# Three pairs of feed-forward blocks per half computed by seven products instead of eight, interleaved with ordinary blocks

## The chip, the core and the metric

The kernel runs on one core of one Trainium2 chip. The metric is device time of one execution in microseconds (us). Engines are named as in the profile: PE multiplies (its weight loads are shown as PEld), DVE, ACT and POOL compute on 128 partitions, SP only issues transfers.

## What is computed

A decoder trunk of two layers over 512 tokens of width 1024. Each layer adds a mixing block (three kinds of token mixer with gates), and then a feed-forward block:

```python
for l in range(DEPTH):
    h = rms_norm(x, mix_norm_g[l])
    ...                                   # three mixers, gated, merged
    x = x + merged @ w_o[l]
    h = rms_norm(x, ffn_norm_g[l])
    x = x + (jax.nn.silu(h @ ffn_w1[l]) * (h @ ffn_w3[l])) @ ffn_w2[l]
```

The feed-forward block's inner width is 2816 = 22 blocks of 128. Everything is float32.

## The kernel before

Activations stand with features on partitions and the 512 tokens along the free side, so one matrix product of a 128x128 weight block with an activation chunk is one matmul of 512 columns. Float32 accuracy comes from splitting every operand into a high and a low part, both in the reduced format fp32r: `split` (L99) makes the high part on ACT (L100) and the low part, source minus high, on DVE or POOL (L101). `mm3` (L111) then issues three matmuls per 128-block: high by high (L113), high by low (L114), low by high (L115). `weights` (L103) loads a raw weight tile of up to 512 columns (four blocks) through SP into one of 3 `wr` buffers and splits it into `wh` and `wl` (4 buffers each); it does so at a raised priority of 90 places, so that loads and splits run ahead of the matmuls. `gemm_gen` (L121) runs one output block over all its input blocks and yields after every second one; `gemm_fm` runs it through. Which instruction goes next on an engine is set at build time by a list scheduler that takes, among those it holds ready, the one traced first; on the chip each engine then works through its list in order.

`ffn` (L1031) works in two halves of 11 inner blocks (`HH`). For each block it runs a product with `w1` (24 matmuls: 8 input blocks by 3) and one with `w3` (24), multiplies the first by the norm factor `rb` (L339), applies tanh on ACT (L1044), two fused operations on DVE (L1045, L1046, the second with `rb` again), multiplies by the `w3` product (L1049), and splits the result into the tiles that `w2` reads. After 11 blocks come 8 products with `w2` (33 matmuls each) whose results are added to `x` (L1055). The norm factor itself is computed late: the sums of squares are reduced by PE behind the first `w1` product (L317) and spread by four transposes in `norm_end` (L331). POOL does nothing in this stage. Ahead of it, `layer` runs the eight output products of `w_o` (24 matmuls each) with `x` updated at L1232, and `norm_chunk` (L299) scales, splits and squares each finished chunk.

PSUM has 8 banks: 2 called `mm`, 2 `s`, 3 `t`, 1 `o`. In this stage an `mm` request takes banks of the first three kinds in turn (`WIDE`). SBUF buffers are counted by tag in `bufs` (L74); `e` and `P3` have 3 each, `big` 6.

Of the kernel before, what the change touches and what calls it, by code (L numbers as in the profile page):

```python
# [19 lines left out]
D, S, L, KC, NT = 1024, 512, 2, 8, 4  # L20
# [4 lines left out]
FFN, HC, HH = 2816, 22, 11  # L25
# [38 lines left out]
class Builder:  # L64
    def __init__(self, ctx, tc, io, layers=L, dbg=None):
        self.tc, self.nc, self.io, self.layers = tc, tc.nc, io, layers
        self.dbg = dbg or {}
        nc = self.nc
        self.V, self.A, self.T = nc.vector, nc.scalar, nc.tensor
        pool = lambda n, b=1, **k: ctx.enter_context(tc.tile_pool(name=n, bufs=b, **k))  # L70
        self.cst, self.sb, self.sm = pool("cst"), pool("sb"), pool("sm", 2)
        self.psum = pool("psum", 1, space=PSUM)
        self.n = 0
        self.bufs = dict(wr=3, wh=4, wl=4, h=16, mg=8, oT=8, cq=10, qk=8, v=8, big=6, pt=5, P0=2, P1=2, P2=2, P3=3, e=3)  # L74
        self.pending = False
        self.pbufs = dict(mm=2, s=2, t=3, o=1)
        self.wide, self.turn = False, 0
        self.weng, self.debt, self.mid = None, 0.0, False
# [287 lines left out]
    def add(self, gen, us, due):  # L366
        self.fillers.append([gen, us, due])
# [641 lines left out]
    def rglru(self, l, fill):  # L1009
# [18 lines left out]
        while outs:  # L1028
            self.rg_out(l, *outs.pop(0))

    def ffn(self, l, x, out_chunk):  # L1031
        V, A, io = self.V, self.A, self.io
        tags = ["oT"] * 8 + ["cq"] * 7 + ["qk"] * 7
        for half in range(2):
            hid = []
            for c in range(HH):
                hc = half * HH + c
                ps1 = self.gemm_fm(io["w1"][l, hc], self.h)
                if c == 0 and half == 0:
                    self.norm_stats()  # L1040
                    ps = self.gemm_fm(io["w3"][l, hc], self.h)
                u = self.rs_mul(ps1)
                th = self.pg("e")
                A.activation(th, u, AF.Tanh, scale=0.5)  # L1044
                V.scalar_tensor_tensor(u, th, 1.0, u, OP.add, OP.mult)  # L1045
                V.scalar_tensor_tensor(u, u, 0.5, self.rb, OP.mult, OP.mult)  # L1046
                if c or half:
                    ps = self.gemm_fm(io["w3"][l, hc], self.h)
                V.tensor_tensor(u, ps, u, OP.mult)  # L1049
                hi, lo = self.pg(tags[2 * c], F32R), self.pg(tags[2 * c + 1], F32R)  # L1050
                self.split(hi, lo, u)
                hid.append((hi, lo))
            for oc in range(KC):
                ps = self.gemm_fm(io["w2"][l, half, oc], hid)
                V.tensor_tensor(x[oc], ps, x[oc], OP.add)  # L1055
                if half == 1:
                    out_chunk(oc, x[oc])

    def run(self):
        nc, V, A, io = self.nc, self.V, self.A, self.io  # L1060
# [17 lines left out]
    def layer(self, l):  # L1078
        nc, V, A, io = self.nc, self.V, self.A, self.io
# [128 lines left out]
        for h in range(1, 8):  # L1208
            g = 48 + 3 * h - 2
# [26 lines left out]
        if not last:
            self.vectors(l + 1)
# [65 lines left out]


def build(d, layers=L, dbg=None):
    nc = bacc.Bacc("TRN2", target_bir_lowering=False, num_devices=1)
    io = {k: nc.dram_tensor(k, v.shape, mybir.dt.from_np(v.dtype), kind="ExternalInput").ap() for k, v in d.items()}
    io["out"] = nc.dram_tensor("out", (KC, 128, S), F32, kind="ExternalOutput").ap()
    io["xs"] = nc.dram_tensor("xs", (KC, 128, S), F32, kind="Internal").ap()
    for k, s in (dbg or {}).items():  # L1310
        io[k] = nc.dram_tensor(k, s, F32, kind="ExternalOutput").ap()
    with tile.TileContext(nc) as tc, ExitStack() as ctx:
        b = Builder(ctx, tc, io, layers, dbg)
        b.run()
    return nc
# [9 lines left out]
```

## Time and profile before

| | us |
|---|---|
| median of 3 runs | 1986.11 (1983.62 to 1986.47) |
| the profiled execution | 1982.81 |
| its span in the trace | 1981.0 |
| PE busy in the span | 1935.6 |
| DVE, ACT, POOL busy | 1319.7, 996.6, 252.0 |

The span is what the trace covers; the remaining 1.8 us of that execution lie around it. A PE row's duration runs from its start to the end of its drain, so that matmuls overlap in the rows; the pace of PE is read from the distances between starts.

### The profile page before, as it was taken

The numbers are of one execution on the slowest core, as the hardware profiler recorded it, in microseconds if no ns is written. First come the engines' busy times: TensorE is split into PE (matmuls) and PEld (weight loads), VectorE is DVE, ScalarE is ACT, GpSimd is POOL, SyncE is SP. The second block draws the span as 40 slices with busy tenths as digits, with TensorE's granted clock in tenths as the row PEclk, the third lists the DMA queues.
The fourth block names the chain that finished last, engine by engine and source line by source line (L and its number), as shares of the span: only waits on it lengthen the run. The fifth ranks groups of instructions, "written<-read, shape, count | busy, mean of one in ns | idle before, by whom it ended". The sixth has DMA issues, their size and how long they took to land.

```text
span 1981.0 us, 26967 instructions
## 1 busy us (share of the span) xinstructions
PE 1935.6 (98%) x9472; PEld 1627.8 (82%) x9472; DVE 1319.7 (67%) x2783; ACT 996.6 (50%) x1937; POOL 252.0 (13%) x232
## 2 busy tenths in 40 slices
PE   9898999999999999999999899999999999999999
PEld 8777878888888888888888688888888888888887
DVE  8689998788545554455556999878874465534542
ACT  5466776687334332233344577857773343323331
POOL 0453442000000000000004536310000000000000
PEclk9999999999999999999999999999999999999999
DMA  5211101223333223323432111113233322333333
GB/s 159 86 56 34 41 31 43 87 94 104 109 125 101 96 96 93 99 98 96 131 112 93 43 41 44 38 46 100 95 102 119 121 91 100 96 94 99 97 102 100
DMA packets 100519, 173.94 MB, mean 88 GB/s; under 512 B 11936, under 2 KB 26144, under 8 KB 100384
## 3 DMA queue, kind: packets, MB, share of 16 engines
q1 hardware_dynamic: 100384, 172.22, 27.3%
q8 instruction: 74, 1.21, 0.2%
q14 instruction: 61, 0.50, 0.1%
HBM read 167.98 MB, written 4.19 MB: 87 GB/s over the span
## 4 chain that ended last, share of the span: by engine, by line
PE 78%; DVE 8%; ACT 2%; issue 1%; POOL 0%; ACTq 0%; DVEq 0%; POOLq 0%
PE pst L114 9%; PE pst L113 9%; PE pst L115 9%; PE psmm L113 8%; PE psmm L114 8%; PE psmm L115 8%; PE pss L114 7%; PE pss L113 7%; PE pss L115 7%; PE pst L660 1%; DVE P L645 1%; DVE pss L633 1%; PE pso L673 1%; PE pso L674 1%; ACT P L636 1%
## 5 line engine op out<-in xcount | busy, mean ns | idle before, releaser
L100 ACT ACTIVATE wh<-wr 128x512 fp32r<-128x512 f32 (+3 forms) x640 | 387.5, 608 | 698.4 <-PE pst L114 261.0
L101 DVE TENSOR_TENSOR wl<-wr,wh 128x512 fp32r<-128x512 f32 (+2 forms) x526 | 355.1, 676 | 247.5 <-ACT wh L100 242.4
L101 POOL TENSOR_TENSOR wl<-wr,wh 128x512 fp32r<-128x512 f32 (+2 forms) x114 | 138.8, 1224 | 951.8 <-ACT wh L100 935.8
L113 PE MATMUL psmm<-h,wh 128*128 128x512 f32 x600 | 237.2, 395 | 3.7 <-ACT wh L100 2.8
L115 PE MATMUL psmm<-h,wl 128*128 128x512 f32 x600 | 235.2, 392 | 0.6 <-POOL wl L101 0.6
L114 PE MATMUL psmm<-h,wh 128*128 128x512 f32 x600 | 235.0, 392 | 0.0
L113 PE MATMUL pst<-h,wh 128*128 128x512 f32 x512 | 199.8, 390 | 0.0
L114 PE MATMUL pst<-h,wh 128*128 128x512 f32 x512 | 199.3, 389 | 0.0
L115 PE MATMUL pst<-h,wl 128*128 128x512 f32 x512 | 199.3, 389 | 0.0
L113 PEld LDWEIGHTS psmm<-h,wh 128*128 128x128 f32 x600 | 112.9, 188 | 26.4 <-ACT wh L100 3.2
L113 PE MATMUL pss<-h,wh 128*128 128x512 f32 x344 | 134.2, 390 | 0.0
L115 PE MATMUL pss<-h,wl 128*128 128x512 f32 x344 | 133.9, 389 | 0.0
L114 PE MATMUL pss<-h,wh 128*128 128x512 f32 x344 | 133.9, 389 | 0.0
L115 PEld LDWEIGHTS psmm<-h,wl 128*128 128x128 f32 x600 | 112.9, 188 | 24.6 <-POOL wl L101 1.1
L114 PEld LDWEIGHTS psmm<-h,wh 128*128 128x128 f32 x600 | 112.9, 188 | 20.8
L636 ACT ACTIVATE P<-pss,nm 128x512 f32<-128x512 f32 x192 | 100.1, 525 | 55.4 <-DVE nm L633 32.3
L113 PEld LDWEIGHTS pst<-h,wh 128*128 128x128 f32 x512 | 96.1, 188 | 20.2 <-ACT e L984 0.4
L115 PEld LDWEIGHTS pst<-h,wl 128*128 128x128 f32 x512 | 96.1, 188 | 20.1
L114 PEld LDWEIGHTS pst<-h,wh 128*128 128x128 f32 x512 | 96.1, 188 | 19.8
L633 DVE CUSTOM_DVE_ANT_0 pss<-pss,mask 128x512 f32<-128x512 f32 x192 | 93.7, 489 | 7.2 <-PE pss L115 5.8
L660 PE MATMUL pst<-ident,P 128*128 128x128 f32 x480 | 76.6, 274 | 11.5 <-DVE P L645 5.3
L660 PEld LDWEIGHTS pst<-ident,P 128*128 128x128 f32 x480 | 58.2, 141 | 28.1 <-issue 17.8
(423 smaller groups left out, 4303.4 us busy)
## 6 DMA issues: line engine op xcount, KB each, us to landing
wr<-w SPq DMA_DIRECT2D x240, 256.0 KB, 2.6
wr<-wfm SPq DMA_DIRECT2D x188, 256.0 KB, 2.6
wr<-wpc SPq DMA_DIRECT2D x32, 256.0 KB, 2.6
wr<-wo SPq DMA_DIRECT2D x32, 256.0 KB, 2.6
wr<-wb SPq DMA_DIRECT2D x32, 192.0 KB, 2.4
wr<-w SPq DMA_DIRECT2D x32, 192.0 KB, 2.3
mg<-xT SPq DMA_DIRECT2D x16, 256.0 KB, 2.7
wr<-wpa SPq DMA_DIRECT2D x16, 256.0 KB, 2.6
```

The lines of the kernel that those rows point to most:

```text
L100: self.A.activation(hi, src, AF.Copy)
L101: (eng or self.V).tensor_tensor(lo, src, hi.bitcast(F32), OP.subtract)
L113: mm(ps, a[0], b[0], start=first, stop=False)
L114: mm(ps, a[0], b[1], start=False, stop=False)
L115: mm(ps, a[1], b[0], start=False, stop=last)
L633: self.V.tensor_tensor_reduce(p[:, :W], p[:, :W], self.mask[:, 512 - W:], 1.0, 3e38, OP.add, OP.min, j.nm[:, i:i + 1])
L636: self.A.activation(j.Pi[i], p[:, :128 * (i + 1)], AF.Exp, bias=j.nm[:, i:i + 1], scale=-1.0, accum_out=j.l[:, i:i + 1])
L645: V.tensor_scalar(j.Pi[i], j.Pi[i], j.gate[:, i:i + 1], j.l[:, i:i + 1], op0=OP.mult, op1=OP.mult)
L660: self.T.transpose(ps[:, c:c + 128], j.Pi[i][:, kt * 128:kt * 128 + 128], self.ident)
L673: T.matmul(o[:, 512 - n:], j.V[kt], h[:, m0:m0 + n], start=j.first and kt == 0, stop=False)
L674: T.matmul(o[:, 512 - n:], j.V[kt], l_[:, m0:m0 + n], start=False, stop=j.last and kt == NT - 1)
```

## The change

Six of the 11 inner blocks of each half are taken as three pairs, each pair with both of its products (`w1` and `w3`) computed by the Strassen-Winograd scheme: the weight is cut into 2x2 parts (two inner blocks by two halves of the 8 input blocks) and the activations into 2x2 parts (two halves of the input blocks by two halves of the tokens), and seven products of 4 blocks by 256 tokens take the place of eight. A pair takes 7 products x 2 matrices x 4 blocks x 3 matmuls = 168 matmuls of 256 columns, where it took 96 of 512. The weight sums `s1` to `s4` are made on POOL, the activation sums `t1` to `t4` on DVE and POOL while `w_o` still runs (`x_scaled`, `x_sums`), and the seven results are combined on DVE as they leave PSUM. The steps of a pair are interleaved with the steps of the five ordinary blocks: one step of an ordinary product (6 matmuls of 512), one step of a pair (12 of 256). The last `w3`-side use of the norm factor moves behind `w2`: the hidden tile is left without it, and each `w2` result is multiplied by `rb` before it is added to `x`. Buffers: `wh` and `wl` 5 each, a new tag `cf`, and the hidden tiles lie under other tags; a smaller scratch area makes room.

```diff
-        self.bufs = dict(wr=3, wh=4, wl=4, h=16, ...
+        self.bufs = dict(wr=3, cf=3, wh=5, wl=5, h=16, ...
+LAS = 2
+DUO_BANKS = ("s", "t", "s", "t", "t")
...
+    def x_sums(self, k, x, g):
+        V, P = self.V, self.nc.gpsimd
+        h, g1 = self.hg[k], g[:, k + 4:k + 5]
+        a, b = slice(0, 256), slice(256, 512)
+        t13, t24 = self.pg("pt"), self.pg("pt")
+        P.tensor_tensor(t13[:, a], h[:, b], h[:, a], OP.subtract)
+        V.scalar_tensor_tensor(t13[:, b], x[:, b], g1, h[:, b], OP.mult, OP.subtract)
+        P.tensor_tensor(t24[:, a], t13[:, b], h[:, a], OP.add)
+        V.scalar_tensor_tensor(t24[:, b], x[:, a], g1, t24[:, a], OP.mult, OP.subtract)
...
+        for t, e in ((t13, V), (t24, P)):
+            hi, lo = self.pg("qk", F32R), self.pg("oT", F32R)
+            self.split(hi, lo, t, e)
...
+    def duo_events(self, srcs):
...
+            ev += [(o - 8, load, o, "r21", "big"), (o - 8, load, o, "r22", "P3"), (o - 7, load, o, "r11", "big"),
+                   (o - 5, add, o, "s1", "r21", "r22", OP.add), (o - 4, load, o, "r12", "big"),
+                   (o - 4, add, o, "s3", "r11", "r21", OP.subtract, "r21"),
+                   (o - 1, add, o, "s2", "s1", "r11", OP.subtract, "r11"),
+                   (o + 2, add, o, "s4", "r12", "s2", OP.subtract, "s2")]
...
+    DUO = (("r11", "b11"), ("s2", "t2"), ("r12", "b21"), ("s1", "t1"), ("s3", "t3"), ("s4", "b22"), ("r22", "t4"))
...
+                ps = self.ps(DUO_BANKS[(7 * u + i) % 5])
+                for m in range(2):
+                    emit(n * u + 2 * i + m)
+                    wh, wl = splits.pop((u, 2 * i + m))
+                    for k in range(4):
+                        s = slice(k * 128, k * 128 + 128)
+                        self.mm3(ps[:, m * 256:m * 256 + 256], (wh[:, s], wl[:, s]), X[xn][k], k == 0, k == 3)
+                    if m == 0:
+                        yield
+                if name == "r11":
+                    A.activation(t1, ps, AF.Copy)
+                elif name == "s2":
+                    V.tensor_tensor(t2, ps, t1, OP.add)
...
+                if name in ("s4", "r22"):
+                    q = int(name == "r22")
+                    late.append(lambda q=q, u=u, f=(f1, f2)[q]: done(u, q, f))
+                yield
...
+    def duo_split(self, splits, key, w, name):
+        hi, lo = self.pg("wh", F32R), self.pg("wl", F32R)
+        self.split(hi, lo, w[name], self.nc.gpsimd if key[1] in (7, 9, 11) else None)
...
+        def hidden(hc, w1, w3, v=lambda t: t):
...
+            V.tensor_tensor(u, w1, v(self.rb), OP.mult)
+            A.activation(th, u, AF.Tanh, scale=0.5)
+            V.scalar_tensor_tensor(u, th, 1.0, u, OP.add, OP.mult)
+            V.scalar_tensor_tensor(u, u, 0.5, w3, OP.mult, OP.mult)
+            A.activation(v(hi), u, AF.Copy)
+            V.tensor_tensor(v(lo), u, v(hi).bitcast(F32), OP.subtract)
...
+        def mix(g, c):
+            while next(c, self) is not self:
+                next(g, None)
+            self.drain(g)
+
+        def down(half, oc):
+            ps = self.gemm_fm(io["w2"][l, half, oc], [self.hid[c] for c in range(HH)])
+            t = self.pg("cf", F32, [128, 2, 512])[:, 0]
+            V.tensor_tensor(t, ps, self.rb, OP.mult)
+            (V if half else self.nc.gpsimd).tensor_tensor(x[oc], x[oc], t, OP.add)
...
+            g = pairs([o + 5, o + 7, o + 9])
+            c = singles(range(o, o + 5))
...
+            self.hid = {}
+            for _ in range(4):
+                next(c)
+            mix(g, c)
...
+            self.x_scaled(oc, t, self.ffng)
+            if oc > 3:
+                self.x_sums(oc - 4, t, self.ffng)
```

## Rows read from the trace of the kernel before

**Rows 1.** The page: span, busy time by engine, chain that ended last by engine.

```profile
span 1981.0 us, 26967 instructions
...
PE 1935.6 (98%) x9472; PEld 1627.8 (82%) x9472; DVE 1319.7 (67%) x2783; ACT 996.6 (50%) x1937; POOL 252.0 (13%) x232
...
PE 78%; DVE 8%; ACT 2%; issue 1%; POOL 0%; ACTq 0%; DVEq 0%; POOLq 0%
```

**Rows 2.** Busy time by stretch (w_o; feed-forward of layers 0 and 1).

```profile
596.00:640.00 44.00, 44.00 (x196) 36.42 (x195) 26.22 (x40) 19.89 (x32) 0.00 (x0) 1.00 0.32 105
645.00:1019.00 374.00, 374.00 (x1673) 311.75 (x1672) 189.46 (x303) 125.60 (x203) 0.00 (x0) 1.00 0.33 105
1622.00:1980.00 358.00, 355.21 (x1573) 293.91 (x1571) 171.99 (x269) 109.52 (x176) 0.00 (x0) 1.00 0.31 98
```

**Rows 3.** PE in order: start, duration; feed-forward of layer 0, first and last.

```profile
639.54 0.39 PE L113 MATMUL pst<-h,wh 128*128 128x512 f32 x1
...
644.75 0.39 PE L115 MATMUL pst<-h,wl 128*128 128x512 f32 x1
644.98 0.95 PE L317 MATMUL pso<-ones,e 128*128 128x1 f32 x8
...
1000.01 0.33 PE L113 MATMUL pst<-wh,h 128*128 128x384 f32 x1
```

**Rows 4.** PE in order: twelve matmuls of 256 columns, and the next.

```profile
278.32 0.28 PE L113 MATMUL psmm<-wh,cq 128*128 128x256 f32 x1
278.44 0.28 PE L114 MATMUL psmm<-wl,cq 128*128 128x256 f32 x1
...
279.75 0.40 PE L113 MATMUL pss<-qk,qk 96*128 96x512 f32 x1
```

**Rows 5.** Weight loads of the same stretch, in order.

```profile
278.44 0.19 PEld L115 LDWEIGHTS psmm<-wh,cq 128*128 128x128 f32 x1
...
279.51 0.19 PEld L115 LDWEIGHTS psmm<-wh,cq 128*128 128x128 f32 x1
```

**Rows 6.** DVE groups of the feed-forward of layer 0: busy us, mean ns.

```profile
L101 DVE TENSOR_TENSOR wl<-wr,wh 128x512 fp32r<-128x512 f32 x134 | 89.9, 671 | 81.7 <-ACT wh L100 79.8 <-PE pso L331 2.0
L1045 DVE SCALAR_TENSOR_TENSOR e<-e,e 128x512 f32<-128x512 f32 x22 | 15.2, 693 | 4.6 <-ACT e L1044 4.5
L1046 DVE SCALAR_TENSOR_TENSOR e<-e,rsb 128x512 f32<-128x512 f32 x22 | 15.2, 692 | 0.7
...
L339 DVE TENSOR_TENSOR e<-psmm,rsb 128x512 f32<-128x512 f32 x8 | 5.5, 691 | 10.8 <-PE psmm L115 10.8
```

**Rows 7.** ACT groups of the same stretch.

```profile
L100 ACT ACTIVATE wh<-wr 128x512 fp32r<-128x512 f32 x134 | 82.9, 619 | 217.6 <-PE pst L114 90.4 <-PE pss L114 64.1 <-PE psmm L114 59.1
L1044 ACT ACTIVATE e<-e 128x512 f32<-128x512 f32 x22 | 13.9, 634 | 8.8 <-DVE e L339 8.8
```

**Rows 8.** POOL groups of the whole span, by shape.

```profile
L101 POOL TENSOR_TENSOR wl<-wr,wh 128x512 fp32r<-128x512 f32 x70 | 93.1, 1334 | 162.7 <-ACT wh L100 151.6 <-PE psmm L114 5.2 <-PE pst L544 3.1
...
L885 POOL TENSOR_TENSOR big<-big,gB 128x512 f32<-128x512 f32 x8 | 10.3, 1293 | 0.0
...
L844 POOL TENSOR_TENSOR big<-big,e 128x256 f32<-128x256 f32 x8 | 6.1, 762 | 0.2
```

**Rows 9.** DVE and POOL at the same moment, both reading two SBUF tiles.

```profile
339.92 1.60 DVE L101 TENSOR_TENSOR wl<-wr,wh 128x512 fp32r<-128x512 f32 x1
...
339.69 1.29 POOL L101 TENSOR_TENSOR cq<-e,cq 128x512 fp32r<-128x512 f32 x1 [14.25 <-ACT cq L100]
```

**Rows 10.** The same, DVE reading one tile from PSUM.

```profile
245.15 0.68 DVE L101 TENSOR_TENSOR pt<-pst,pt 128x512 fp32r<-128x512 f32 x1
...
244.72 1.26 POOL L101 TENSOR_TENSOR wl<-wr,wh 128x512 fp32r<-128x512 f32 x1
```

**Rows 11.** DVE in order: the chain of one hidden block.

```profile
690.13 0.69 DVE L339 TENSOR_TENSOR e<-pss,rsb 128x512 f32<-128x512 f32 x1 [1.54 <-PE pss L115]
...
691.58 0.69 DVE L1045 SCALAR_TENSOR_TENSOR e<-e,e 128x512 f32<-128x512 f32 x1 [0.16 <-ACT e L1044]
692.31 0.69 DVE L1046 SCALAR_TENSOR_TENSOR e<-e,rsb 128x512 f32<-128x512 f32 x1
...
695.57 0.69 DVE L1049 TENSOR_TENSOR e<-psmm,e 128x512 f32<-128x512 f32 x1 [1.54 <-PE psmm L115]
...
696.96 0.69 DVE L101 TENSOR_TENSOR cq<-e,cq 128x512 fp32r<-128x512 f32 x1
```

**Rows 12.** The end of the span: last matmul and last operation.

```profile
1976.82 0.39 PE L115 MATMUL psmm<-qk,wl 128*128 128x512 f32 x1
1977.25 0.69 DVE L1055 TENSOR_TENSOR mg<-psmm,mg 128x512 f32<-128x512 f32 x1 [6.79 <-PE psmm L115]
```

**Rows 13.** Waits in the feed-forward of layer 0: us in total, times, longest.

```profile
ACT wh L100 <- PE pst L114: 90.4, 53, 2.2
DVE wl L101 <- ACT wh L100: 79.8, 73, 2.0
```

More of the change, by code (lines that the diff above doesn't have):

```diff
@@ L73, in __init__ @@
         self.n = 0
-        self.bufs = dict(wr=3, wh=4, wl=4, h=16, mg=8, oT=8, cq=10, qk=8, v=8, big=6, pt=5, P0=2, P1=2, P2=2, P3=3, e=3)
+        self.bufs = dict(wr=3, cf=3, wh=5, wl=5, h=16, mg=8, oT=8, cq=10, qk=8, v=8, big=6, pt=5, P0=2, P1=2, P2=2, P3=3, e=3)
         self.pending = False
@@ L1029, in rglru, with x_scaled @@
             self.rg_out(l, *outs.pop(0))
+    def x_scaled(self, k, x, g):
+        if k < 4:
+            if k % 2 == 0:
+                self.hp = self.pg("cf", F32, [128, 2, 512])
+            t = self.hp[:, k % 2]
+            self.A.activation(t, x, AF.Copy, scale=g[:, k:k + 1])
+            self.hg.append(t)
+    def x_sums(self, k, x, g):
[7 more added lines that the diff above has]
+        V.scalar_tensor_tensor(t24[:, b], x[:, a], g1, t24[:, a], OP.mult, OP.subtract)
+        out = []
+        for t, e in ((t13, V), (t24, P)):
+            hi, lo = self.pg("qk", F32R), self.pg("oT", F32R)
+            self.split(hi, lo, t, e)
+            out.append((hi, lo))
+        self.tx.append(out)
@@ new lines, in x_parts @@
+    def x_parts(self):
+        a, b = slice(0, 256), slice(256, 512)
+        cut = lambda p, s: (p[0][:, s], p[1][:, s])
+        h, tx = self.h, self.tx
+        return dict(b11=[cut(h[k], a) for k in range(4)], b21=[cut(h[k + 4], a) for k in range(4)],
+                    b22=[cut(h[k + 4], b) for k in range(4)],
+                    t1=[cut(tx[k][0], a) for k in range(4)], t3=[cut(tx[k][0], b) for k in range(4)],
+                    t2=[cut(tx[k][1], a) for k in range(4)], t4=[cut(tx[k][1], b) for k in range(4)])
@@ new lines, in duo_events, with load, add @@
+    def duo_events(self, srcs):
+        P, D = self.nc.gpsimd, self.nc.sync.dma_start
+        W = [{}, {}]
+        def load(m, name, tag):
+            f, q = int(name[1]) - 1, int(name[2]) - 1
+            t = W[m][name] = self.pg(tag, F32, [128, 768])[:, :512] if tag == "big" else self.pg(tag)
+            D(t, srcs[m][f][:, q * 512:q * 512 + 512])
+        def add(m, out, a, b, op, into=None):
+            w = W[m]
+            w[out] = w[into] if into else self.pg("e")
+            P.tensor_tensor(w[out], w[a], w[b], op)
+        ev = []
+        for o in (0, 1):
+            ev += [(o - 8, load, o, "r21", "big"), (o - 8, load, o, "r22", "P3"), (o - 7, load, o, "r11", "big"),
[3 more added lines that the diff above has]
+                   (o + 2, add, o, "s4", "r12", "s2", OP.subtract, "s2")]
+        return W, ev
@@ new lines, with duos, emit @@
+    DUO = (("r11", "b11"), ("s2", "t2"), ("r12", "b21"), ("s1", "t1"), ("s3", "t3"), ("s4", "b22"), ("r22", "t4"))
+    def duos(self, units, X, done):
+        V, A = self.V, self.A
+        n, at = 14, {}
+        splits = {}
+        for u, srcs in enumerate(units):
+            W, ev = self.duo_events(srcs)
+            for e in ev:
+                at.setdefault(n * u + e[0], []).append(e[1:])
+            for p in range(n):
+                at.setdefault(n * u + p - LAS, []).append((self.duo_split, splits, (u, p), W[p % 2], self.DUO[p // 2][0]))
+        keys = sorted(at)
+        late = []
+        def emit(g):
+            while keys and keys[0] <= g:
+                for f, *a in at[keys.pop(0)]:
+                    f(*a)
+        emit(-LAS)
+        yield
+        for u in range(len(units)):
+            f1, f2 = (self.pg("cf", F32, [128, 2, 512]) for _ in range(2))
+            t1, t3, t2, t4 = f1[:, 0], f1[:, 1], f2[:, 0], f2[:, 1]
+            for i, (name, xn) in enumerate(self.DUO):
+                ps = self.ps(DUO_BANKS[(7 * u + i) % 5])
[11 more added lines that the diff above has]
+                    V.tensor_tensor(t2, ps, t1, OP.add)
+                elif name == "r12":
+                    V.tensor_tensor(t1, ps, t1, OP.add)
+                elif name == "s1":
+                    V.tensor_tensor(t3, ps, t2, OP.add)
+                elif name == "s3":
+                    V.tensor_tensor(t4, ps, t3, OP.add)
+                    V.tensor_tensor(t2, ps, t2, OP.add)
+                elif name == "s4":
+                    V.tensor_tensor(t3, ps, t3, OP.add)
+                else:
+                    V.tensor_tensor(t2, ps, t2, OP.add)
+                for f in late:
+                    f()
+                late = []
+                if name in ("s4", "r22"):
+                    q = int(name == "r22")
+                    late.append(lambda q=q, u=u, f=(f1, f2)[q]: done(u, q, f))
+                yield
+        for f in late:
+            f()
@@ L1031, in ffn @@
+    def duo_split(self, splits, key, w, name):
+        hi, lo = self.pg("wh", F32R), self.pg("wl", F32R)
+        self.split(hi, lo, w[name], self.nc.gpsimd if key[1] in (7, 9, 11) else None)
+        splits[key] = hi, lo
     def ffn(self, l, x, out_chunk):
         V, A, io = self.V, self.A, self.io
-        tags = ["oT"] * 8 + ["cq"] * 7 + ["qk"] * 7
-        for half in range(2):
[L1035 to L1057, printed above, removed]
@@ new lines, in ffn @@
+        tags = ["cq"] * 10 + ["v"] * 8 + ["pt"] * 4
+        X = self.x_parts()
+        cut = lambda t: t.rearrange("p (a t) -> p a t", a=2)
+        def hidden(hc, w1, w3, v=lambda t: t):
+            c = hc % HH
+            hi, lo = self.pg(tags[2 * c], F32R), self.pg(tags[2 * c + 1], F32R)
+            th, u = v(self.pg("e")), w1
+            V.tensor_tensor(u, w1, v(self.rb), OP.mult)
[4 more added lines that the diff above has]
+            V.tensor_tensor(v(lo), u, v(hi).bitcast(F32), OP.subtract)
+            self.hid[c] = hi, lo
@@ new lines, in singles @@
+        def singles(cs):
+            for hc in cs:
+                ps1 = yield from self.gemm_gen(io["w1"][l, hc], self.h)
+                u = self.pg("P3")
+                A.activation(u, ps1, AF.Copy)
+                if hc == 0:
+                    self.norm_stats()
+                yield
+                ps = yield from self.gemm_gen(io["w3"][l, hc], self.h)
+                if self.pending:
+                    self.norm_end()
+                hidden(hc, u, ps)
+                yield
@@ new lines, in pairs @@
+        def pairs(cs):
+            units = [[[io[w][l, c], io[w][l, c + 1]] for w in ("w1", "w3")] for c in cs]
+            return self.duos(units, X, lambda u, q, f: hidden(cs[u] + q, f[:, :, 0:256], f[:, :, 256:512], cut))
+        def mix(g, c):
[7 more added lines that the diff above has]
+            (V if half else self.nc.gpsimd).tensor_tensor(x[oc], x[oc], t, OP.add)
@@ new lines, in ffn @@
+        for half in range(2):
+            o = half * HH
+            g = pairs([o + 5, o + 7, o + 9])
+            c = singles(range(o, o + 5))
+            if half:
+                for oc in range(KC):
+                    if oc == 6:
+                        next(g)
+                    down(0, oc)
+            else:
+                next(g)
+            self.hid = {}
+            for _ in range(4):
+                next(c)
+            mix(g, c)
+        for oc in range(KC):
+            down(1, oc)
+            out_chunk(oc, x[oc])
@@ L1227, in layer @@
         self.norm_begin()
+        self.hg, self.tx = [], []
         for oc in range(KC):
@@ L1305, in build @@
 def build(d, layers=L, dbg=None):
-    nc = bacc.Bacc("TRN2", target_bir_lowering=False, num_devices=1)
+    nc = bacc.Bacc("TRN2", target_bir_lowering=False, num_devices=1, dynamic_dma_scratch_size=1024)
     io = {k: nc.dram_tensor(k, v.shape, mybir.dt.from_np(v.dtype), kind="ExternalInput").ap() for k, v in d.items()}
```

## The prediction

> **What bounds the kernel now.** Read the busy shares and the chain first [rows 1]: PE is busy 1935.6 of 1981.0 us and holds 78% of the chain that ended last. Then read the stage that changes [rows 2]: from 645 to 1019 us PE is busy in all of the 374.00 us, DVE in 189 (51%), ACT in 126, POOL in none. The feed-forward is bound by the number and pace of matmuls alone; the waits there are of ACT for PE to free a weight buffer, and of DVE for ACT [rows 13], so splits run as far ahead as buffers allow. Last, read PE's pace from starts, not durations [rows 3]: 23 intervals from 639.54 to 644.75 are 0.2265 us each, though one row lasts 0.39. The feed-forward of layer 0 runs from 639.54 to 1000.01; 1584 matmuls of 0.2265 are 358.8 of these 360.5 us, so it holds 1.7 us of anything else. Matmuls removed there are time removed, as long as nothing new makes PE wait.
>
> **What PE gains.** A matmul of 256 columns has the same 128x128 weight load ahead of it, so its pace must be read, not halved. Twelve in a row start from 278.32 to 279.75, 0.1192 each [rows 4], 5% more than half of 0.2265. Their weight loads follow each other as closely, 9 intervals in 1.07 us [rows 5]; the rows show no gap. A pair took 96 x 0.2265 = 21.74 us and will take 168 x 0.1192 = 20.03: 1.72 us less, not the eighth of 2.7 that the count promises. There are 12 pairs (3 per half, 2 halves, 2 layers): **20.6 us** gained. Starts are read to 0.01 us over 12 intervals, 0.0008 each; over 2016 matmuls that is 1.7, so 19 to 22. At 0.1294 per matmul the gain would be gone.
>
> **What is added, and its cover.** One half's interleaved part is 240 x 0.2265 = 54.4 us of ordinary blocks and 60.1 of pairs: 114.5 us. Its splits: 20 weight tiles of ordinary blocks and 42 of pairs (14 per pair, where 8 stood), 9 of these on POOL. DVE then does 53 low parts, 21 combinations of PSUM results, and 44 operations of hidden blocks (4 each; 5 before, since `rb` moves behind `w2`): 118 operations of 0.69 [rows 6] or 81 us, 71%. ACT does 62 high parts, 22 for hidden blocks, 5 copies and 3 first combinations, 92 x 0.63 [rows 7] = 58 us, 51%. POOL does 24 weight sums and 9 low parts at 1.29 [rows 8]: 43 us. Bytes loaded do not change. Taken alone each engine is covered by PE.
>
> They are not alone. A DVE low part that starts while POOL works on two SBUF tiles took 1.60 us instead of 0.69, and ended about 0.5 after POOL did [rows 9]; a DVE operation that reads one input from PSUM took 0.68 beside POOL [rows 10]. So POOL's time and that of DVE operations on two SBUF tiles add up. Of the 118, 26 read PSUM (21 combinations, 5 ordinary `w3` factors); the other 92 take 63.5 us, and with POOL's 42.6 that is **106 of 114.5 us**, 93%. The Trainium skill says the same on its page SBUF — State Buffer, section "SBUF: two separate sides": the pair of ports that both engines use is a lock, held for the whole instruction, and the loser blocks. The trace agrees with it here (1.60 against 0.69); taken to its end the rule gives the second rival below.
>
> At 93% the average is covered and the bursts decide. Steps alternate: one of an ordinary block (6 x 0.2265 = 1.36) and one of a pair (12 x 0.1192 = 1.43), 2.79 us together. Each pair of steps wants a pair's split, and splits are traced 2 steps ahead (`LAS`), 5.6 us, of which the chain high part, low part takes about 1.4. That leaves some 4 us of cover. Four costs follow, with both ends:
>
> - *Joints inside a half* (8): as two hidden blocks of a finished pair come due, two steps want 4 hidden operations, 2 low parts and 2 of ordinary blocks (8 x 0.69) and a POOL sum (1.29), 6.8 us in 5.6, twice in a row: 2.4 us late, under the cover of 4. In-order queues may add. 0 to 2 each; I take 0.4, near the covered end, since `e` tiles (3, two held by `s1`) only delay hidden blocks that nobody on PE needs yet: 3.
> - *Ends of halves* (4): no ordinary steps are left for the last 6 steps of the third pair, and its last two hidden blocks are needed by the first `w2` product after 27 matmuls, 6.1 us, and 30, 6.8. Behind the last matmul stand one combination, 8 hidden operations and 2 low parts for `w2`, 11 x 0.69 = 7.6, with tanh and a copy between: 8 to 10 us late for the second block. In the trace before, one product and one split follow the last matmul, 2.1 us [rows 11], under the same cover. PE waits 0 (if the next `w2` product is ordered ahead) to 3.5; I take 1.2: 5.
> - *Start of each feed-forward* (2): for four `w_o` products DVE's 3.3 us per 5.5 (26.2 over 8 [rows 2]) grow by some 1.6 (an operation of 512 and two of 256), and POOL adds 1.29 + 2 x 0.76 [rows 8]: about 1.5 us late per product, 6 in all. The activation sums are first needed some 12 us into the stage. 0 to 4; I take 1: 2. POOL and DVE wait for each other within one sum; the `w_o` low parts queue behind.
> - *End of the kernel*: the last operation, 0.69 after the last matmul [rows 12], becomes two: 0.7. In the first half of `w2` this second addition goes to POOL, idle then: nothing.
>
> On SP the pairs' loads wait for `big` and `P3` tiles, and the ordinary blocks' loads queue behind; 3 `wr` tiles hold 3 x 5.6 us of ordinary work, so a wait of one or two steps is hidden. A fifth `wh` and `wl` in the rest of the kernel may move PE's 45 us of idle [rows 1] by a few either way; I take 0, ends -3 and +3.
>
> **The sum.** -20.6 + 3 + 5 + 2 + 0.7 = -10. Against the profiled 1982.8 that is 1973; the median shown is 3.3 above it, so 1986.1 - 10 = **1976**.
>
> **The rivals.**
> (1) All is covered: only the last 0.7 is paid, 1986.1 - 20 = 1966. For it: the stage's slack before, 1.7 us in 360. Against it: 93%, and the ends of halves.
> (2) The lock becomes the bound, slower than before. If POOL's 42.6 us are never hidden behind DVE's PSUM operations, the interleaved part takes 81.4 + 42.6 = 124 instead of 114.5: 9.5 per half, 38 in all, 1986 - 20.6 + 38 = 2003. It decides as soon as the lock costs PE over 5.2 us per half, when about half of POOL's time meets a blocked DVE with no slack behind. For it: [rows 9], with nothing of the kind in this stage before, and buffers for two steps only. Against it: a DVE that waits for ACT or PE has idle time in which POOL runs.
> (3) Buffers, not engines: `r22` holds two of three `P3` tiles nearly always, and an ordinary `w1` result is copied into the third; if the next `r22` takes it, a PSUM bank is held four steps longer and PE waits for a bank. About 2 us per pair, 12 pairs, eats the gain but for my other costs: about 1986, no change. The trace before shows no such wait; nothing excludes it.
> That fewer matmuls are issued than told is no case: the count is fixed by the code.
>
> **How the numbers follow.** Forecast (1971 to 1982) 0.44; rival 1, 0.20; rival 2, between 1988 and 2003, 0.20; rival 3, 0.16. A measurement of this kernel can tell about 0.2%, 4 us: same is 1982 to 1990. Faster: 0.43 + 0.20 + 0.02 = 0.65. Same: 0.01 + 0.02 + 0.13 = 0.16. Slower: 0.18 + 0.01 = 0.19. The range of 8 in 10 runs from 1964 to 1998.
>
> **What the profile of the changed kernel would show.** Starts of 256-column matmuls 0.119 apart over whole pairs with 1008 of 512 and 1008 of 256 columns per layer (1584 - 6 x 96 and 6 x 168) show the first step right. PE idle ahead of pair matmuls, released by DVE or POOL low parts, is the lock; ahead of the first `w2` product, released by the last hidden tile, is the end of a half; ahead of a product's first matmul, released by ACT's copy or a DVE combination, is a bank. DVE low parts well above 0.69 in the stage show the lock whatever it costs. A pace over 0.13 in pairs, or a feed-forward over 360 us, would make the prediction wrong.

## The result and the profile after

The changed kernel takes **2011.95 us** (2010.81 to 2012.68, 4 runs) against 1985.59 before (the three runs of the table above and a fourth, 1985.07): 1.0134 times, interval 1.0116 to 1.0151. It is slower by 26 us, where 10 us less was forecast, and lies outside the range. Its profiled execution took 2010.81, with a span of 2009.0.

The page after (busy time by engine, POOL's busy tenths in 40 slices, the chain that ended last; it answers to [rows 1]):

```profile
span 2009.0 us, 29244 instructions
...
PE 1934.9 (96%) x10336; PEld 1657.1 (82%) x10336; DVE 1455.8 (72%) x2899; ACT 1061.9 (53%) x2065; POOL 503.7 (25%) x404
...
POOL 0453531000004332333004626300000053323410
...
PE 68%; DVE 15%; ACT 3%; issue 2%; POOL 1%; DMA 0%; POOLq 0%; ACTq 0%; DVEq 0%
```

PE is busy as long as before (1934.9 against 1935.6) in a span 28 us longer, and its share of the chain falls from 78% to 68%; DVE's rises from 8% to 15%. POOL, empty in the feed-forward before, now works in it (slices 13 to 19 and 33 to 39, counted from 1).

The first step of the forecast held. PE in order, layer 0 (start, duration, idle before and what ended it; it answers to [rows 3] and [rows 4]):

```profile
648.74 0.28 PE L115 MATMUL pss<-h,wh 128*128 128x256 f32 x1
...
650.05 0.28 PE L117 MATMUL pss<-h,wl 128*128 128x256 f32 x1
...
652.52 0.54 PE L115 MATMUL pss<-h,wh 128*128 128x512 f32 x1 [2.19 <-ACT wh L102]
652.86 0.63 PE L116 MATMUL pss<-h,wh 128*128 128x512 f32 x1
657.23 0.80 PE L117 MATMUL pss<-h,wl 128*128 128x512 f32 x1 [3.74 <-DVE wl L103]
657.82 0.63 PE L115 MATMUL pss<-h,wh 128*128 128x512 f32 x1
...
659.10 0.42 PE L115 MATMUL pst<-qk,wh 128*128 128x256 f32 x1
659.31 0.42 PE L116 MATMUL pst<-oT,wh 128*128 128x256 f32 x1
...
696.15 0.50 PE L117 MATMUL pss<-h,wl 128*128 128x512 f32 x1 [1.48 <-DVE wl L103]
```

From 648.74 to 650.05 there are 11 intervals of a pair's matmuls, 0.1191 each, as forecast (0.1192), and layer 0's trace has 1008 of them. The time goes between them: 2.19 us before 652.52, 3.74 before 657.23, 1.48 before 696.15, each ended by a high or a low part. Behind the first two the pace itself drops: 657.82 to 659.10 is 0.43 per matmul of 512 columns and 0.21 per one of 256, twice the normal, until about 664. The granted clock says the same (columns: stretch; PE, PEld, DVE, ACT, POOL busy; clock; DMA share, GB/s):

```profile
637.00:700.00 63.00, 55.01 (x315) 47.45 (x313) 45.05 (x61) 23.10 (x39) 30.41 (x23) 0.92 0.21 67
700.00:760.00 60.00, 58.09 (x368) 51.77 (x367) 43.84 (x59) 28.36 (x48) 21.40 (x14) 1.00 0.30 96
```

The mean of 0.92 over 63 us is full clock (2.4 GHz) but for some 10 us at the lower level (1.2 GHz), which fits the long rows from 652.86 to 664: PE had stood still for 2.19 us ahead of them, and did so for 3.74 among them.

Adding up, stretch by stretch, how much later each start comes than the pace of 0.2265 and 0.1192 gives (stretches over 0.3 us) closes the account. For example 650.05 to 652.86 is 2.81, less 0.12 and 0.23: 2.46 lost.

| lost by PE, us | layer 0 | layer 1 | forecast, both |
|---|---|---|---|
| start of the feed-forward | 11.1 | 9.9 | 2 |
| joints and inside the interleaved parts | 10.6 | 10.3 | 3 |
| ends of halves | 5.0 | 3.1 | 5 |
| sum | 26.7 | 23.3 | 10 |

50 us lost less 20.6 gained is 29.4; the span grew by 28.0, and the feed-forward of layer 0 starts 2.5 us earlier than before (637.08 against 639.54). In the kernel before, the same count gives 0.4 us per layer.

**Who is late.** The start, on POOL, ACT and DVE (three views, in order of time; columns as above):

```profile
647.82 1.62 POOL L1078 TENSOR_TENSOR big<-big,big 128x512 f32<-128x512 f32 x1
649.52 1.28 POOL L1078 TENSOR_TENSOR big<-e,big 128x512 f32<-128x512 f32 x1
...
651.98 2.97 POOL L1078 TENSOR_TENSOR big<-big,big 128x512 f32<-128x512 f32 x2
```

```profile
650.83 0.63 ACT L102 ACTIVATE wh<-big 128x512 fp32r<-128x512 f32 x1 [3.60 <-POOL big L1078]
...
651.85 0.62 ACT L102 ACTIVATE wh<-wr 128x512 fp32r<-128x512 f32 x1
```

```profile
648.40 1.07 DVE L155 TENSOR_SCALAR ni<-nv 128x4 int32<-128x4 int32 x1
...
652.50 1.25 DVE L156 TENSOR_SCALAR ny<-ni 128x4 int32<-128x4 int32 x1
653.78 1.18 DVE L159 TENSOR_TENSOR nt<-ny 128x4 f32<-128x4 f32 x1
...
656.37 0.16 DVE L161 SCALAR_TENSOR_TENSOR ny<-nt,ny 128x4 f32<-128x4 f32 x1
656.48 0.69 DVE L103 TENSOR_TENSOR wl<-wr,wh 128x512 fp32r<-128x512 f32 x1
```

POOL makes the first pair's sums among the activation sums, 1.3 to 1.7 us each. ACT waits 3.60 for one of them, and the ordinary block's high part (651.85) stands behind that in ACT's queue. DVE's norm chain, operations on 128x4 that take 0.16 a little later, takes 1.07 to 1.25 beside POOL, and the low part that PE waits for (656.48) stands behind it.

A joint, the same three engines:

```profile
689.81 1.74 POOL L1078 TENSOR_TENSOR big<-e,big 128x512 f32<-128x512 f32 x1
691.51 1.74 POOL L1078 TENSOR_TENSOR big<-big,big 128x512 f32<-128x512 f32 x1
693.33 1.62 POOL L1078 TENSOR_TENSOR big<-e,big 128x512 f32<-128x512 f32 x1
```

```profile
690.32 1.77 DVE L103 TENSOR_TENSOR wl<-big,wh 128x512 fp32r<-128x512 f32 x1
...
692.61 1.19 DVE L1165 TENSOR_TENSOR cf<-cf,rsb 128x512 f32<-128x512 f32 x1
693.72 1.77 DVE L1170 TENSOR_TENSOR cq<-P,cq 128x512 fp32r<-128x512 f32 x1
695.41 0.68 DVE L103 TENSOR_TENSOR wl<-wr,wh 128x512 fp32r<-128x512 f32 x1
```

```profile
692.73 0.63 ACT L1169 ACTIVATE cq<-P 128x512 fp32r<-128x512 f32 x1 [3.83 <-DVE P L1168]
693.26 0.61 ACT L102 ACTIVATE wh<-wr 128x512 fp32r<-128x512 f32 x1
```

DVE's operations on two SBUF tiles take 1.2 to 1.8 us here, beside POOL's sums. The two engines take turns: POOL's sums start 1.70 us apart (689.81, 691.51), and DVE finishes one such operation in that time (690.32), where it needs 0.69 alone. No engine at this joint waits for a POOL sum; DVE's own operations are late. The hidden block's chain is late by that, ACT waits 3.83 in its queue for it, the ordinary block's high part follows only at 693.26 and its low part, behind a 1.77, at 695.41: PE waits until 696.15.

The groups of DVE and POOL in the feed-forward of layer 0 (mean ns of one; they answer to [rows 6] and [rows 8]):

```profile
L103 DVE TENSOR_TENSOR wl<-wr,wh 128x512 fp32r<-128x512 f32 x68 | 51.4, 757 | 61.6 <-ACT wh L102 61.0
L103 DVE TENSOR_TENSOR wl<-big,wh 128x512 fp32r<-128x512 f32 x47 | 40.1, 858 | 20.3 <-ACT wh L102 20.1
...
L1139 DVE TENSOR_TENSOR cf<-pst,cf 128x512 f32<-128x512 f32 x4 | 2.7, 682 | 0.0
```

```profile
L1078 POOL TENSOR_TENSOR big<-big,big 128x512 f32<-128x512 f32 x24 | 39.4, 1650 | 19.5 <-issue 10.0 <-DVE wl L103 9.0
...
L1078 POOL TENSOR_TENSOR e<-big,P 128x512 f32<-128x512 f32 x12 | 17.5, 1461 | 46.4 <-DMA P<-w 18.6 <-issue 12.7 <-DVE wl L103 11.4
```

Low parts take 757 and 858 where the same shape took 688 before ([rows 6] take all widths together: 671; the row below, of the kernel before from 645 to 1000 us, takes 512 columns alone); a combination that reads PSUM (L1139) still takes 682. POOL's sums take 1461 to 1650, not the 1290 that I had used: POOL is held up as well.

```profile
L101 DVE TENSOR_TENSOR wl<-wr,wh 128x512 fp32r<-128x512 f32 x117 | 80.5, 688 | 54.4 <-ACT wh L100 52.4 <-PE pso L331 2.0
```

### The profile page after: what moved, and what is told of

Same layout as the page of the kernel before. It is cut to its first block, busy times and chain, and to the rows that moved or that the text cites. A ratio compares the mean times of both kernels' runs of the same rounds, so it can differ in the third digit from the quotient of the medians.

```text
span 2009.0 us, 29244 instructions
## 1 busy us (share of the span) xinstructions
PE 1934.9 (96%) x10336; PEld 1657.1 (82%) x10336; DVE 1455.8 (72%) x2899; ACT 1061.9 (53%) x2065; POOL 503.7 (25%) x404
## 4 chain that ended last, share of the span: by engine, by line
PE 68%; DVE 15%; ACT 3%; issue 2%; POOL 1%; DMA 0%; POOLq 0%; ACTq 0%; DVEq 0%
PE pst L117 9%; PE pst L116 9%; PE pst L115 9%; PE psmm L115 6%; PE psmm L116 6%; PE psmm L117 6%; PE pss L117 6%; PE pss L116 6%; PE pss L115 6%; DVE wl L103 3%; DVE P L647 1%; PE pst L662 1%; DVE pss L635 1%; PE pso L675 1%; PE pso L676 1%
## 5 line engine op out<-in xcount | busy, mean ns | idle before, releaser
L102 ACT ACTIVATE wh<-wr 128x512 fp32r<-128x512 f32 (+3 forms) x544 | 326.9, 603 | 472.8 <-PE pst L116 180.3
L103 DVE TENSOR_TENSOR wl<-wr,wh 128x512 fp32r<-128x512 f32 (+2 forms) x430 | 299.1, 697 | 224.0 <-ACT wh L102 221.8
L117 PE MATMUL pst<-h,wl 128*128 128x512 f32 (+1 forms) x520 | 189.4, 364 | 5.1 <-DVE wl L103 5.1
L115 PE MATMUL psmm<-h,wh 128*128 128x512 f32 x480 | 191.4, 399 | 2.7 <-DVE chid L468 2.5
L115 PE MATMUL pst<-h,wh 128*128 128x512 f32 (+1 forms) x520 | 189.9, 365 | 0.3
L116 PE MATMUL pst<-h,wh 128*128 128x512 f32 (+1 forms) x520 | 189.6, 365 | 0.3 <-DVE h L305 0.3
L117 PE MATMUL psmm<-h,wl 128*128 128x512 f32 x480 | 188.4, 392 | 0.9 <-DVE wl L103 0.9
L116 PE MATMUL psmm<-h,wh 128*128 128x512 f32 x480 | 188.7, 393 | 0.0
L117 PE MATMUL pss<-h,wl 128*128 128x512 f32 (+1 forms) x360 | 125.5, 349 | 16.5 <-DVE wl L103 16.5
L115 PE MATMUL pss<-h,wh 128*128 128x512 f32 (+1 forms) x360 | 125.1, 347 | 4.5 <-ACT wh L102 4.4
L116 PE MATMUL pss<-h,wh 128*128 128x512 f32 (+1 forms) x360 | 124.5, 346 | 0.0
L102 ACT ACTIVATE wh<-big 128x512 fp32r<-128x512 f32 x120 | 74.8, 629 | 79.8 <-PE pst L116 22.3
L103 DVE TENSOR_TENSOR wl<-big,wh 128x512 fp32r<-128x512 f32 x96 | 83.1, 871 | 40.0 <-ACT wh L102 39.7
L115 PEld LDWEIGHTS psmm<-h,wh 128*128 128x128 f32 x480 | 90.8, 189 | 19.3 <-DVE chid L468 3.2
L116 PEld LDWEIGHTS psmm<-h,wh 128*128 128x128 f32 x480 | 90.8, 189 | 14.4
```

The lines of the kernel that those rows point to most:

```text
L102: self.A.activation(hi, src, AF.Copy)
L103: (eng or self.V).tensor_tensor(lo, src, hi.bitcast(F32), OP.subtract)
L115: mm(ps, a[0], b[0], start=first, stop=False)
L116: mm(ps, a[0], b[1], start=False, stop=False)
L117: mm(ps, a[1], b[0], start=False, stop=last)
```

## The experiments

Theories: **lock** (POOL's work on SBUF and DVE's exclude each other, and PE's losses are this exclusion, carried on by in-order queues); **own load** (DVE simply has too much in bursts for a lookahead of two steps); **slow server** (splits wait for sums that POOL makes late). All numbers of "lost" are worked out as in the table above, one number a layer (layer 0 where only one is given). Each kernel was run once, except the last two (4 runs each); the kernel before took 1982.8 to 1986.3 beside them.

**Without the weight sums.**

```diff
-  (o - 5, add, o, "s1", "r21", "r22", OP.add) ...
+  (o - 5, same, o, "s1") ...        # split the raw part instead; also s2, s3, s4
```

> The changed kernel without the weight sums s1 to s4 on POOL: raw weight parts are split in their place, so the output is not the reference's. DVE and ACT keep every operation (118 DVE operations per half between w_o and w2), POOL keeps only the 9 low parts per half. Theory lock (POOL operations on two SBUF tiles shut DVE out): POOL's share falls by 24 x 1.3 to 1.65 us per half, DVE low parts come down to about 0.70, the stalls of about 1.4 us at the joints between pairs (21 us in both layers) nearly vanish (under 4 us), and part of the 21 us lost at the two starts goes too; total 1975 to 1985. Theory own load (DVE's bursts alone are too much for a lookahead of two steps, POOL does not matter): joints stay within 4 us of 21, total over 2000.

Measured: 1965.81, lost 1.1 in layer 0, low parts 689 ns. All of the loss hangs on the sums, more than lock's own forecast had it; own load is out, since DVE kept its 118 operations per half. Whether the sums hurt by excluding DVE or by being late, this run doesn't tell.

**The weight sums on DVE.**

```diff
-        P, D = self.nc.gpsimd, self.nc.sync.dma_start
+        P, D = self.V, self.nc.sync.dma_start
```

> The changed kernel with the 24 weight sums per half on DVE instead of POOL, nothing left out. DVE has 142 operations x 0.69 = 98 us of 114.5 per half, POOL 9 low parts (12 us). Theory lock: the sum of what excludes each other falls from 106 to about 92 us, DVE operations come down to 0.69 to 0.75, losses at starts and joints shrink by a third to two thirds, total 1985 to 2002. Theory own load: 17 us more of DVE per half make every joint worse, total 2012 or more.

Measured: 1968.54, below the range that I gave for lock. The feed-forward of layer 0 by engine, of the changed kernel first, then of this one (columns as above), and this one's DVE groups:

```profile
640.00:1000.00 360.00, 343.67 (x1948) 298.33 (x1947) 232.98 (x322) 141.98 (x239) 112.97 (x76) 0.98 0.30 94
```

```profile
640.00:1000.00 360.00, 359.62 (x2062) 316.44 (x2061) 248.35 (x399) 152.53 (x256) 40.69 (x29) 1.00 0.34 102
```

```profile
L103 DVE TENSOR_TENSOR wl<-wr,wh 128x512 fp32r<-128x512 f32 x72 | 49.5, 688 | 43.2 <-ACT wh L102 42.9
L103 DVE TENSOR_TENSOR wl<-big,wh 128x512 fp32r<-128x512 f32 x47 | 32.6, 697 | 14.5 <-ACT wh L102 14.4
...
L1078 DVE TENSOR_TENSOR e<-big,P 128x512 f32<-128x512 f32 x12 | 10.4, 874 | 9.3 <-DMA P<-w 9.2
```

DVE does more (248 against 233 us busy in the stretch) and PE loses 1.9 us instead of 26.7. Low parts are back at 688 and 697. DVE even waits 9.2 us for the late loads of `r22`, at no cost to PE. Own load is refuted a second time, with the sign reversed.

**Without the activation sums.**

```diff
-            self.x_scaled(oc, t, self.ffng)
-            if oc > 3:
-                self.x_sums(oc - 4, t, self.ffng)
...
+        tx = [(h[k], h[k + 4]) for k in range(4)]
```

> The changed kernel without the activation sums t1 to t4 (x_scaled and x_sums left out, scaled chunks read in their place, so the output is not the reference's). The products with w_o then have before's DVE work and no POOL. Theory backlog (the sums fall behind during w_o and push the norm chain and the first low parts late): the loss at each start falls from 10 to 11 us to under 3, total 1994 to 1998, joints unchanged at about 21 us. Theory first pair (the first pair's own weight sums on POOL, and ACT and DVE queued behind them, make the loss): starts keep at least 6 us each, total 2002 to 2012.

Measured: 1993.42. Each start loses 1.8 (11.1 and 9.9 in the changed kernel); joints and ends stay: 14.4 and 14.1 in the two layers, against 15.6 and 13.4. With the run before this says that the loss at the start needs both, the first pair's weight sums on POOL and the activation sums; without either of them the start is covered. This run leaves out all work on the activation sums, DVE's and ACT's as well as POOL's, and doesn't tell which of it counts.

**The norm factor alone**, in the kernel before.

```diff
-                V.scalar_tensor_tensor(u, u, 0.5, self.rb, OP.mult, OP.mult)
...
-                V.tensor_tensor(u, ps, u, OP.mult)
+                V.scalar_tensor_tensor(u, u, 0.5, ps, OP.mult, OP.mult)
...
+                V.tensor_tensor(t, ps, self.rb, OP.mult)
+                (V if half else self.nc.gpsimd).tensor_tensor(x[oc], x[oc], t, OP.add)
```

> The kernel before with one part of the change alone: the second factor rb moves behind w2, on POOL's add in the first half, no pairs and no sums. One DVE operation less per block (44 x 0.69 = 30 us of DVE in all), 32 multiplications by rb more (22 us). PE waits for none of them. All theories: within 2 us of before, the end 0.7 us later.

Measured: 1983.96 beside 1986.18 for the kernel before on the same chip, one run each: no part of the loss.

**Unrelated work on POOL beside the sums on DVE.** Three kernels; the added line is an addition, an index pattern, or a copy into a scratch tile:

```diff
+            self.nc.gpsimd.tensor_tensor(self.junk, self.mask, self.mask, OP.add)
```

> The kernel with the weight sums on DVE (1968.5 us), and beside each of them an addition of 128x512 on POOL that reads two SBUF operands and writes a scratch tile nobody reads or waits for: 96 of 1.3 us or so, as many as the sums that POOL did in the changed kernel. Theory lock (POOL shuts DVE out while it works): DVE operations on two SBUF tiles stretch to 0.8 to 1.2 us in the mean and PE stalls come back at starts and joints, though nothing depends on POOL; DVE holds 98 us of 114.5 per half and some 30 of POOL's come on top, so total 2000 to 2040, worse than the changed kernel. Theory slow server (in the changed kernel the splits waited for sums that POOL made slowly, DVE was not shut out): 1967 to 1971.

> The same with an operation of 128x512 on POOL that reads nothing (an index pattern written into the scratch tile), 96 of an estimated 0.5 to 1 us. If POOL shuts DVE out only while it reads: DVE means stay at 0.69 and the total is 1967 to 1972. If any POOL work does: 1975 to 2010.

> The same with a POOL copy of 128x512, one SBUF operand read. If reading is what excludes DVE, one operand is enough and losses come back in proportion to the copy's time: 1975 to 2020. If it takes two operands: 1967 to 1972.

Measured: 2004.01 with additions, 1968.52 with patterns, 1969.42 with copies. The numbers look like lock, but the runs missed their place: nothing in the added operations depends on the stage, and they were ordered ahead, into the attention stage (first at 281 us, the last of layer 0 ending at 345). The feed-forward kept its 2 us of loss in all three, and in attention POOL's real low parts queue behind 48 additions, so the 35 us there may be a queue as well as a lock. They count for one thing only, the duration of a POOL addition (of one tile with itself) and of a POOL copy of 128x512 that are seldom held (count, then min, median, max ns):

```profile
L1079 POOL TENSOR_TENSOR pct<-mask x96: 1029/1039/1373, 281.8 to 1335.1; 128x512 f32<-128x512 f32 x96
```

```profile
L1079 POOL COPY pct<-mask x96: 603/615/966, 280.9 to 1296.5; 128x512 f32<-128x512 f32 x96
```

**POOL additions and copies in place.** The same, tied to the stage by reading the sum that DVE has just made; nobody waits for the result.

```diff
+            self.nc.gpsimd.tensor_tensor(self.junk, w[out], self.mask, OP.add)
```

> The kernel with all weight sums on DVE (1968.5 us), and behind each sum a POOL addition of 128x512 that reads this sum and a constant and writes a scratch tile nobody waits for: 24 per half as in the changed kernel, now in the interleaved part itself (in the earlier run with unrelated additions they all ran in the attention stage, so it told nothing of this part). Only the reuse of the scratch tile ties POOL to itself. Theory lock: DVE has 98 us and 24 x 1.1 to 1.3 of POOL come on top, 92 + 28 = 120 us of 114.5, so starts and joints lose again: 1995 to 2030, DVE means 0.75 to 0.95. Theory slow server (splits waited for sums that POOL made late): nothing on the path waits for POOL, 1967 to 1972.

Measured: 2023.86, worse than the changed kernel; lost 29.6 and 30.5. This run separates the two theories: POOL's result is needed by nobody, no split waits for it, and the loss is back. It loads the stage more than the changed kernel does, though (120 us of 114.5 by the count above, against 106). DVE's group, then one place on DVE, POOL and PE:

```profile
L103 DVE TENSOR_TENSOR wl<-wr,wh 128x512 fp32r<-128x512 f32 x67 | 59.0, 881 | 33.4 <-ACT wh L102 33.0
```

```profile
881.50 1.75 DVE L103 TENSOR_TENSOR wl<-wr,wh 128x512 fp32r<-128x512 f32 x1
```

```profile
881.12 1.59 POOL L1079 TENSOR_TENSOR pct<-big,mask 128x512 f32<-128x512 f32 x1 [0.69 <-DVE big L1078]
...
891.71 6.43 POOL L1079 TENSOR_TENSOR pct<-big,mask 128x512 f32<-128x512 f32 x1 [4.30 <-DVE big L1078]
```

```profile
883.31 0.50 PE L117 MATMUL pss<-h,wl 128*128 128x512 f32 x1 [1.40 <-DVE wl L103]
```

The low part takes 1.75 beside POOL's addition and PE stands still for it, 1.40 us before 883.31. The additions that read `big` tiles, in the whole span (count, then min, median, max ns):

```profile
L1079 POOL TENSOR_TENSOR pct<-big,mask x72: 1284/1612/6439, 649.1 to 1939.1; 128x512 f32<-128x512 f32 x72
```

A POOL addition that meets a row of DVE operations took 6.43 where the shortest took 1.28 (spans on POOL are rough). In the trace no engine waits for any of the 96. Slow server as the only cause is refuted; that lateness adds nothing in the changed kernel is not shown by this run.

> The same with a POOL copy of the sum (one SBUF operand, about 0.62 us) in place of the addition. If one operand read by POOL excludes DVE's two-operand work: 24 x 0.62 = 15 us per half more, 92 + 15 = 107 of 114.5 as in the changed kernel, 1985 to 2012. If only two do: 1967 to 1973 and DVE means of 0.69.

Measured: 1978.59, lost 8.3 and 9.6; low parts of ordinary blocks 748 ns.

```profile
L1079 POOL COPY pct<-big 128x512 f32<-128x512 f32 x36 | 52.0, 1445 | 56.1 <-DVE big L1078 53.6 <-DVE ny L161 1.3 <-DVE nt L160 0.7
```

```profile
L103 DVE TENSOR_TENSOR wl<-wr,wh 128x512 fp32r<-128x512 f32 x71 | 53.1, 748 | 41.1 <-ACT wh L102 40.8
```

One operand read by POOL is enough, and the copies are held too: 1445 ns in the mean, against 615. The loss is a third of that of the additions, though by the sum of times (107 of 114.5) it should have matched the changed kernel.

**Half of the sums on DVE.**

```diff
-            P.tensor_tensor(w[out], w[a], w[b], op)
+            (self.V if out in ("s1", "s2") else P).tensor_tensor(w[out], w[a], w[b], op)
```

> The changed kernel with s1 and s2 on DVE and s3 and s4 on POOL, nothing left out. Per half DVE has 130 operations (90 us) and POOL 12 sums and 9 low parts (27 us); what excludes each other sums to about 99 us of 114.5 (106 in the changed kernel, 92 with all sums on DVE). If the loss follows the sum in proportion: halfway, 1985 to 1995. If it begins at a threshold, when the sum passes what the lookahead can cover: below 1978.

Measured: 1999.69, lost 19.3 and 16.9: neither of the two. At 92 us of exclusive work in 114.5 the loss is 4 in both layers, at 99 it is 36, at 106 it is 50. It sets in between 92 and 99 and isn't a function of the sum: the copies in place, at 107, lost 18. Here POOL and DVE also wait for each other's sums (DVE 1.18 us for one of POOL's, once at each start).

**No POOL in the stage**, and the sums on DVE timed with it.

```diff
-        self.split(hi, lo, w[name], self.nc.gpsimd if key[1] in (7, 9, 11) else None)
+        self.split(hi, lo, w[name], None)
...                                  # weight sums, x_sums and down's additions on V as well
```

> The changed kernel with everything that POOL does in the feed-forward and during w_o on DVE: weight sums, the 9 low parts per half, activation sums, the additions behind w2. DVE then has 151 operations, 104 us of 114.5 per half, and nothing excludes it. Theory lock: no loss comes back, 1964 to 1970, at or a little below the kernel with only the weight sums on DVE (its feed-forwards lose 1.9 us each). If 91% of DVE is too much for the lookahead: 1972 to 1985.

> The changed kernel with the weight sums on DVE, timed against the kernel before: 1966 to 1971, a ratio of 0.990 to 0.993; 20.6 us of PE time gained, less 3 to 4 at starts and end.

Measured: **1965.61** (1963.96 to 1966.82), 0.9902 times the kernel before, interval 0.9886 to 0.9919; with only the weight sums on DVE 1967.84, 0.9914 times, 0.9899 to 0.9928. The feed-forward of layer 0 without POOL:

```profile
640.00:1000.00 360.00, 359.70 (x2065) 317.00 (x2064) 256.00 (x429) 152.09 (x255) 0.00 (x0) 1.00 0.34 102
```

DVE is busy 71% of this stretch and 91% by count in the interleaved parts, and PE loses 1.9 and 1.5 us. This version beats both kernels, by 20 us and by 46.

**Held time against loss.** The kernel without POOL gives the median duration of each DVE operation and shape undisturbed. The table adds up by how much DVE's rows exceed it in the feed-forward of layer 0 of each kernel (rows more than 0.05 us over).

| kernel | DVE held, us | lost by PE, us |
|---|---|---|
| no POOL in the stage | 0 | 1.9 |
| without the weight sums | 3.9 | 1.1 |
| the weight sums on DVE | 9.0 | 1.9 |
| copies in place | 19.7 | 8.3 |
| half of the sums on DVE | 25.4 | 19.3 |
| without the activation sums | 30.7 | 16.2 |
| the changed kernel | 35.9 | 26.7 |
| additions in place | 50.2 | 29.6 |

The loss goes with the time for which DVE is held, but for one pair of rows; up to 9 us of it cost nothing. The two kernels in which nobody needs POOL's results (copies and additions in place) lie among the others. This is a comparison of eight traces and not an experiment of its own.

## Why the prediction was wrong, point by point

- **PE's gain: right.** 0.1191 per matmul of 256 columns, 20.6 us. The kernel without POOL is 20.2 us below the kernel before, which is what rival 1 (everything covered) gave: 1966.
- **Added work, engine by engine: right** in its counts, and misleading, as the text itself said. POOL's sums were priced at 1.29 from [rows 8]; in the stage they took 1.46 to 1.65. That doesn't raise the 106 us of exclusive work, since a row that is held contains its wait: at the joint above one POOL sum and one DVE operation in turn took 1.70, not 1.29 + 0.69.
- **Joints: the step that failed.** I took 0.4 each, 3 in all, "near the covered end", because 4 us of cover stood against 2.4 of lateness. Measured: 10.6 and 10.3 in the two layers, 20.9 in all. The cover does not exist in this form: while POOL works through its sums, DVE gets one operation on two SBUF tiles per sum, and splits, hidden blocks and the norm chain share ACT's and DVE's in-order queues; a late hidden block, which "nobody on PE needs yet", held ACT for 3.83 us, with the ordinary block's high part behind it. I had looked at the pair's splits, two steps ahead; what PE waited for was the low part of the ordinary block.
- **Start: failed as well**, 2 taken with a bound of 8 for both, 21.0 measured. I counted the lateness of the activation sums (6 us) against their own need (12 us later) and left out that the first pair's sums stand in the same POOL queue, that ACT waits for those with an ordinary high part behind, and that tiny DVE operations of the norm chain are held as long as large ones. The first stop (2.19) hangs on a late POOL sum, the second (3.74) on DVE's held operations. About 3 us of layer 0's 11.1 are the lower clock that followed: 7.12 lost from 652.86 to 664.27, less 4.14 until 657.23.
- **Ends of halves**: 8.1 against 5, within the bound of 14 (4 times 3.5); the end of the kernel is as told (two operations of 0.69 behind the last matmul):

```profile
2004.52 0.69 DVE L1199 TENSOR_TENSOR cf<-pst,rsb 128x512 f32<-128x512 f32 x1 [6.06 <-PE pst L117]
2005.24 0.69 DVE L1200 TENSOR_TENSOR mg<-mg,cf 128x512 f32<-128x512 f32 x1
```

- **Rival 2, the lock as the bound, is what happened**, with the right mechanism (the in-place additions show that it is enough), given 0.20 and at most 2003. Its price was too low since it took only the excess of time over PE's, 9.5 per half, as if the waits came once the sum was full; they come from bursts, before it is: half of the sums on DVE (99 of 114.5) already lost 36.
- **Rival 3**: the late `r22` loads are there (POOL waited 18.6 us for them in layer 0), but no PE wait on a bank was seen, and the runs with the sums on DVE have the same loads and no loss.
- **The rule of the Trainium skill** (SBUF — State Buffer, "SBUF: two separate sides": the shared pair is an exclusive lock, the loser blocks) was named in the forecast and weighed as a rival. The runs bear it out in both directions: DVE's low parts at 757 to 881 ns against 688, a POOL addition at up to 6.43 us against 1.28. The forecast's 93% says neither that the work fits nor what it costs: at the same sum the changed kernel lost 50 and the copies in place 18.

What stays open: how the 50 us divide between exclusion and POOL's lateness. Direct waits for a weight sum on POOL show almost only at the start (ACT, 3.67 and 3.60 us in layer 0, and one of 0.18 later); at joints the trace shows DVE held. The additions in place show that exclusion alone is enough for 60 us; that lateness alone would cost nothing was not tried, since no run made POOL late without making it work. Why half of the sums costs 36, more than its place in the table of held time suggests, is not settled either.

## What to carry to other kernels

Before moving elementwise work from VectorE (DVE) to an idle GpSimd (POOL), add GpSimd's time to VectorE's work on two SBUF tiles in that stage and treat the two as one engine. The sum is a warning and not a price (107 of 114.5 cost 18 us, 106 cost 50); what bursts of GpSimd do to VectorE's operations has to be read from a trace. An idle GpSimd beside a busy VectorE was not free capacity here: VectorE alone, at 91%, was 46 us faster than the two together. Cover by lookahead counts only if nothing that can be late stands ahead of the covered instruction in the same in-order queue. What a restructured product saves depends on the pace of its matmuls at the new width (0.119, where half of 0.2265 is 0.113), which the trace of the kernel before can show ahead of time.

## What the runs showed of the hardware that was not expected

- The exclusion hits small operations as hard as large ones: DVE operations of 128x4, 0.16 us alone, took 1.07 to 1.25 beside a POOL sum. DVE operations with an input from PSUM were not held: in the feed-forward of layer 0 of the changed kernel none of the 69 of 128x512 took over 693 ns.
- It goes both ways: a POOL addition that takes 1.28 at the shortest took 1.61 in the median, 6.43 at one place; a one-operand copy, 0.62 where it was seldom held, took 1.45 in the mean.
- An index pattern written by POOL, 0.56 us each and reading nothing, cost nothing in the attention stage; in the feed-forward it was not tried.
- Stops of 2.19 and 3.74 us cost more than themselves: the granted clock was at its lower level for some 10 us around the second, about 3 us of loss. The many stops of 0.9 to 1.5 us at joints were not followed by it in the changed kernel (1.00 in the second stretch), while one of 1.72 us at the end of a half of layer 0 was (0.74 from 780 to 785).
